# One-core hybrid mLSTM/HGRN2 step: three orders changed on ScalarE and VectorE (weight split, gate set-up, mix blocks of the output projection)

## The chip, the core and the metric

The kernel runs on one core of a Trainium2 chip. Its engines work side by side, each through its own queue of instructions in order: PE (TensorE, matrix multiplication; PEld is its weight load), DVE (VectorE), ACT (ScalarE), POOL (GpSimd) and SP (SyncE, which here issues all DMAs). A semaphore wait at the head of a queue holds everything behind it. The metric is the device time of one execution in microseconds (us), here a median of three runs: 1157.92, from 1155.51 to 1158.99.

## What is computed

One layer of a decoder trunk, on a prompt of 1024 tokens and 8 samples of 8 tokens (T = 1088 columns in all). Cut to what matters:

```python
xn = rmsnorm(x, g_norm)                                # 1024 features
xm, zm, om, fh, qh, ih, zh = split(xn @ w_in, 1024)    # 7 x 1024 outputs

xc = silu(causal_conv(xm, conv_w))                     # mLSTM: 4 heads
q, k, v = xc @ w_q, xc @ w_k, xm @ w_v                 # per head
gates = concat(q, k, v) @ w_gate + b_gate
ig, lf = gates[..., :4], log_sigmoid(gates[..., 4:])
hm, C1, n1, m1 = mlstm_scan(q / sqrt(128), k, v, ig, lf, C0, n0, m0)
hm = (layernorm(hm) * m_ln * sigmoid(om) + m_skip * xc) * silu(zm)

f = lb + (1 - lb) * sigmoid(fh)                        # HGRN2: 8 heads
oh, S1 = hgrn2_scan(silu(qh), (1 - lb) * sigmoid(-fh), ih, log(f), S0)
oh = rmsnorm(oh) * h_norm * silu(zh)

y = rmsnorm(x + concat(hm, oh) @ w_out) * g_final      # 2048 -> 1024
```

## The kernel before

**Exact products.** Each fp32 operand is kept as a rounded high part and the rest (hi, lo). A product takes three multiplications, hi·hi, lo·hi and hi·lo (`mm3`, L94 to L96). A weight block (128 x 1024) is therefore loaded raw by SP (`wraw`), copied to `whi` by ScalarE and subtracted to `wlo` by GpSimd or VectorE (`blk_split`, L147 for both). Raw blocks of W_in, of the per-head weights, of W_out (`woraw`) and of the mixed activations (`mraw`) share three buffers; whi/mhi have two, wlo/mlo two.

**The front.** For each of the four mLSTM heads, `front_conv` projects x_m in three column pieces (`in_block` with its callback: `xmh`/`XB` by ScalarE, `xml` by VectorE), and does the convolution (`Y`, L483 and L486, on VectorE) and SiLU (L492 to L498). `front_v` then computes v and the gates' share of it for nine token tiles, six multiplications each, into three PSUM buffers (tag mm, also used by the projection). ScalarE empties each with two copies: 256 columns to `vt` (L516), 8 to `GTOK` for head 0 or `GST` for the others (L517). `front_qk` computes q and k (L543). `in_block` begins, when it has a single item, with the split of the next weight block: `blk_split(nxt)`.

**Weaves and mixers.** Behind the front, `weave` interleaves projection blocks (the side list) with the mixers of HGRN2 heads and mLSTM heads in turn, H0, M0, H1 and so on to H7. From here on TensorE's order is the one in which the program is written (`manual_schedule`); the other engines' order comes from the scheduler of the framework, which takes dependencies and its own estimate of times, and a call `behind(a, b)` makes a depend on b. `gate_scan` runs beside the first mixer H0: it writes the gates to `gd` in memory and reads them back as `glf`, `gt`, `ig`, `gy` in rows, makes `lm` (4 x 8), sets eight columns of `gt` (MEMSET, L577) and of `gy` (L578), and scans (L579). At the first level H0 makes `Q` and two `K` folds on VectorE (L997, L961), then the copy `Sf` (L1012), and TensorE multiplies `lv` from them (L101).

**The output projection.** W_out is used in two halves of 512 columns, hf = 0 and 1, over token tiles t = 0 to 8 (t = 8 has 64 tokens). For each (hf, t) two groups g = 0, 1 of contraction blocks (8 and 7 blocks, 24 and 21 multiplications) are computed by `out_part`, and the last block by `out_done`, which adds x, sums squares and stores (hf = 0) or normalises and writes out y (hf = 1). `mix_prep(t, g)` loads a group's mixed activations from memory (`mixd`) into `mraw`, splits them on ScalarE (`mhi`, L1302; L1298 for t = 8) and VectorE (`mlo`, L1303). It is called at the head of each out_part, except for the very first group. `early_out` does the parts (0, 0) to (0, 4) within the last weave. What follows is the tail: out_done(0, 0..8) with parts (0, 5) to (0, 8) among them, one `wo_prep(1, i)` (load and split of a block of W_out's second half; `woh` L1276, `wol` L1277) after each of the first six, then the second half in the order 8, 0, 1, ... 7.

Of the kernel before, what the change touches and what calls it, by code (L numbers as in the profile page):

```python
# [17 lines left out]
T = 1088  # L18
# [12 lines left out]
def hybrid_step(  # L31
# [87 lines left out]
    r = 0  # L119
# [50 lines left out]
    def blk_split(i):  # L170
        if i < len(blocks):
            return w_split(("w", i), V if i in v_splits else G)
# [96 lines left out]
    def in_block(*items):  # L269


        ws = []
        for kind, j, evac in items:
            i = bidx[(kind, j)]
            if i > 1 or len(items) == 1:
                if ("w", i) in wq and not isinstance(wq[("w", i)], tuple):
                    blk_split(i)
            ws.append(i)
        for i in ws:
            blk_load(i + 2)  # L280
        nxt = ws[-1] + 1
        if len(items) == 1:
            blk_split(nxt)
        for c, (t0, n) in enumerate(CH):
            xh, xl = xchunk(XH, c), xchunk(XL, c)
            for (kind, j, evac), i in zip(items, ws):
                wh, wl = wq[("w", i)]
                ps = ps_mm()
                for k in range(8):
                    mm3(ps[:, :n], (wh[:, k, :], wl[:, k, :]), (xh[:, k, :], xl[:, k, :]), k == 0, k == 7)  # L290
                    if k % 2 and k < 7:
                        yield cost(6, n)
                evac(c, t0, n, ps)
                yield cost(6, n)
# [206 lines left out]
    def front_v(h):  # L501
        wh, wl = qkv_w[h]
        xms = [fr[2 * h + a]["m"] for a in range(2)]
        for t in range(9):
# [11 lines left out]
            S.copy(vv[:, u, 0:256], ps[:, :256])  # L516
            S.copy((GST if h else GTOK)[:, t, :], ps[:, 256:264])  # L517
            if t == 8:
# [37 lines left out]
    def gate_scan():  # L556
# [18 lines left out]
        lm = small(8, "lm")  # L575
        V.tensor_tensor(lm[0:4, :], lfs, m0t, op=ALU.add)
        V.memset(t1[:, TP:T].rearrange("p (b c) -> p b c", c=8)[:, :, 0], -1e30)  # L577
# [308 lines left out]
    def hgrn_in(h):  # L886
# [36 lines left out]
        else:  # L923
            for i in range(3):
                wo_load(0, i)
            for n, c in enumerate(in_block(("i", h, ev_i), ("z", h, ev_silu(z))), 1):
                if n == 8:
                    for i in range(3):
                        wo_split(0, i)
                    wo_load(0, 3)  # L930
                    ctxs["mix0"] = mix_prep(0, 0, True)
                elif n == 16:
                    wo_split(0, 3)
                yield c
# [6 lines left out]
    def hgrn_main(h):  # L941
# [69 lines left out]
        k2 = fold(K1[:, 512:1024], 1, 1, False)  # L1011
        V.tensor_copy(hv(Sf, T, 1)[:, :, 0, :], hv(f, T, 1)[:, :, 1, :])  # L1012
        G.memset(hv(Sf, T, 1)[:, :, 1, :], 1.0)
# [301 lines left out]

    def out_part(hf, t, g):

# [3 lines left out]
        ps = acc[(hf, t)]  # L1321
        mx = ctxs.pop("mix0") if (hf, t, g) == (0, 0, 0) else mix_prep(t, g)
        for k in range(len(mx)):
# [87 lines left out]
    def early_out():  # L1411
        for t in range(EARLY):
# [5 lines left out]
            if t < STORED:  # L1418
                out_store(t)

    side = chain(*[(hgrn_in if kind == "H" else mlstm_in)(h) for kind, h in jobs], early_out())
    prep = qkv_prep(0)
# [20 lines left out]
    with tc.manual_schedule(engines={mybir.EngineType.PE}):  # L1443
# [8 lines left out]
        weave(side, hgrn_main(7), (us / 2 + EARLY * cost(45, 512)) / HEAD["H"])  # L1452
        for t in range(9):
            out_done(0, t)
            if 3 <= t < 7:
                run(chain(out_part(0, t + 2, 0), out_part(0, t + 2, 1)))
            if t < 6:
                wo_prep(1, t)
        wo_prep(1, 6)
        wo_prep(1, 7)  # L1460
        gf = unit("gf")
        ctxs["gf"] = gf
        nc.sync.dma_start(out=gf[:, :DM], in_=g_final.unsqueeze(0).to_broadcast([P, DM]))
        for t in (8, *range(8)):
            run(chain(out_part(1, t, 0), out_part(1, t, 1)))
            out_done(1, t)
# [87 lines left out]
```

## Time and profile before

| | |
|---|---|
| three runs, median | 1157.92 us (1155.51 to 1158.99) |
| the profiled execution | 1159.27 us, of it 1157.5 us span |
| granted TensorE clock, mean | 0.992 |
| TensorE busy | 1121.6 us |
| VectorE, ScalarE, GpSimd busy | 745.1, 467.9, 259.7 us |
| DMA | 134.05 MB, 116 GB/s over the span |

A profile's timeline row is: start, duration (us), engine, line, operation, output <- inputs, partitions x elements, and how often. Brackets give the idle time of the engine before it and the instruction that ended this idle time. Durations on one engine overlap a little, since an engine begins an instruction while the one ahead drains; so the step from start to start is what counts. Line numbers are those of the kernel before.

### The profile page before, as it was taken

Reading aid. Unit: us, or ns where it says so; the run is one execution under the profiler, and the core shown is the slowest. Engines: PE = TensorE matmul, PEld = TensorE weight load, DVE = VectorE, ACT = ScalarE, POOL = GpSimd, SP = SyncE. Lnnn points to the kernel's source line nnn. Section 1 sums busy time; section 2 is a strip of 40 time slices with the busy share of each in tenths; the row PEclk is TensorE's granted clock in tenths of the full one; section 3 lists DMA queues with packets and bytes.
Section 4 is the critical chain, followed back from the end, with each engine's and each line's share of the span. In section 5 each row is a group of like instructions: output and inputs, shape, how many; then the busy total and the mean of one; then the engine's idle time right before and its main releaser. Section 6 shows DMA issues by size and latency. Waiting matters only on the chain.

```text
span 1157.5 us, 22938 instructions
## 1 busy us (share of the span) xinstructions
PE 1121.6 (97%) x9251; PEld 1055.4 (91%) x9251; DVE 745.1 (64%) x1474; ACT 467.9 (40%) x1045; POOL 259.7 (22%) x403
## 2 busy tenths in 40 slices
PE   5889999999999999999999999999999999999997
PEld 5789999899999999999999999999999997878886
DVE  4665354394778667784779567877676686644543
ACT  5454454434532444235423453252524354333332
POOL 4352443102530044203530153102020200100000
PEclk9889999999999999999999999999999999999999
DMA  7234343213324152323224331422222255576662
GB/s 250 56 122 143 119 144 126 71 50 117 103 76 146 54 167 73 122 94 127 64 78 151 116 112 60 133 76 77 56 77 56 76 175 144 156 215 177 188 190 93
DMA packets 154296, 134.05 MB, mean 116 GB/s; under 512 B 11515, under 2 KB 130391, under 8 KB 154190
## 3 DMA queue, kind: packets, MB, share of 16 engines
q1 hardware_dynamic: 154190, 132.59, 36.6%
q8 instruction: 73, 1.20, 0.4%
q14 instruction: 33, 0.27, 0.1%
HBM read 93.99 MB, written 38.57 MB: 115 GB/s over the span
## 4 chain that ended last, share of the span: by engine, by line
PE 84%; DVE 6%; DMA 5%; ACT 3%; issue 2%; POOL 0%; SPq 0%; POOLq 0%; DVEq 0%; ACTq 0%
PE mm L94 23%; PE mm L95 23%; PE mm L96 23%; PE lv L101 2%; DMA mraw<-mixd 2%; DMA woraw<-in_w_out 2%; PE o L1190 1%; PE o L1209 1%; PE o L94 1%; PE o L96 1%; PE o L95 1%; PE o L1212 1%; DVE mlo L1303 1%; PE lv L1171 1%; PE o L1104 1%
## 5 line engine op out<-in xcount | busy, mean ns | idle before, releaser
L94 PE MATMUL mm<-XH,whi 128*128 128x384 f32 (+1 forms) x1344 | 450.1, 335 | 2.2 <-DVE xml L470 2.0
L95 PE MATMUL mm<-XL,whi 128*128 128x384 f32 (+1 forms) x1344 | 440.0, 327 | 0.0
L96 PE MATMUL mm<-XH,wlo 128*128 128x384 f32 (+1 forms) x1344 | 439.5, 327 | 0.0
L94 PEld LDWEIGHTS mm<-XH,whi 128*128 128x128 f32 x1344 | 253.8, 189 | 4.8 <-DVE xml L470 2.2
L95 PEld LDWEIGHTS mm<-XL,whi 128*128 128x128 f32 x1344 | 253.7, 189 | 1.6 <-issue 1.3
L96 PEld LDWEIGHTS mm<-XH,wlo 128*128 128x128 f32 x1344 | 253.2, 188 | 0.0
L147 POOL TENSOR_TENSOR wlo<-wraw,whi 128x1024 fp32r<-128x1024 f32 x34 | 83.1, 2445 | 104.7 <-ACT whi L147 104.6
L147 ACT CAST whi<-wraw 128x1024 fp32r<-128x1024 f32 x56 | 58.8, 1050 | 94.5 <-PE mm L95 74.6
L948 POOL MEMSET A<- 128x288 f32 x8 | 2.7, 343 | 261.4 <-ACT A L1077 261.4
L1302 ACT CAST mhi<-mraw 128x1024 fp32r<-128x1024 f32 (+1 forms) x32 | 31.8, 997 | 66.5 <-PE mm L95 42.8
L96 PE MATMUL mm<-XH,mlo 128*128 128x512 f32 x144 | 56.5, 392 | 2.1 <-DVE mlo L1303 2.1
L94 PE MATMUL mm<-XH,mhi 128*128 128x512 f32 x144 | 56.9, 395 | 1.2 <-ACT mhi L1302 1.2
L95 PE MATMUL mm<-XL,mhi 128*128 128x512 f32 x144 | 56.1, 390 | 0.0
L1303 DVE TENSOR_TENSOR mlo<-mraw,mhi 128x1024 fp32r<-128x1024 f32 (+1 forms) x32 | 37.0, 1156 | 20.6 <-ACT mhi L1302 19.4
L470 DVE TENSOR_TENSOR xml<-mm,xmh 128x384 fp32r<-128x384 f32 (+1 forms) x24 | 12.3, 511 | 50.9 <-ACT XB L469 47.9
L896 DVE TENSOR_SCALAR f<-f,OML,LB 128x384 f32<-128x384 f32 (+1 forms) x24 | 32.8, 1368 | 12.0 <-ACT f L894 11.6
L1371 POOL TENSOR_TENSOR rs<-rs,mhalf 128x1 f32<-128x1 f32 (+1 forms) x9 | 4.9, 542 | 148.5 <-DVE rs L1370 148.5
L96 PE MATMUL mm<-woh,mlo 128*128 128x512 f32 x96 | 37.5, 390 | 0.1
L95 PE MATMUL mm<-wol,mhi 128*128 128x512 f32 x96 | 37.4, 389 | 0.0
L94 PE MATMUL mm<-woh,mhi 128*128 128x512 f32 x96 | 37.3, 389 | 0.0
L486 DVE SCALAR_TENSOR_TENSOR Y<-XB,PAR,Y 128x1112 f32<-128x1112 f32 x24 | 36.8, 1533 | 0.3
L964 DVE TENSOR_TENSOR QK<-hk,Sf 128x256 f32<-128x256 f32 x96 | 36.2, 419 | 0.0
(355 smaller groups left out, 2188.3 us busy)
## 6 DMA issues: line engine op xcount, KB each, us to landing
wraw<-in_w_in SPq DMA_DIRECT2D x56, 512.0 KB
woraw<-in_w_out SPq DMA_DIRECT2D x16, 512.0 KB
mraw<-mixd SPq DMA_DIRECT2D x16, 512.0 KB
mraw<-mixd SPq DMA_DIRECT2D x16, 448.0 KB
xcd<-XB SPq DMA_DIRECT2D x8, 544.0 KB
qkd<-qk SPq DMA_DIRECT2D x16, 272.0 KB
xcr<-xcd SPq DMA_DIRECT2D x8, 544.0 KB
mixd<-xcr SPq DMA_DIRECT2D x8, 544.0 KB
```

The source lines that it names most:

```text
L94: PE.matmul(out, lhsT=lh, rhs=rh, start=first, stop=False)
L95: PE.matmul(out, lhsT=lh, rhs=rl, start=False, stop=False)
L96: PE.matmul(out, lhsT=ll, rhs=rh, start=False, stop=last)
L101: i = PE.matmul(out, lhsT=lhsT, rhs=rhs, start=start, stop=stop)
L147: return S.copy(hi, raw), eng.tensor_tensor(lo, raw, f32(hi), op=ALU.subtract)
L470: evs.append(V.tensor_tensor(ml[:, t0:t0 + m], ps[:, :m], f32(mh[:, t0:t0 + m]), op=ALU.subtract))
L486: V.scalar_tensor_tensor(Y[:, :1112], XB[:, j:j + 1112], cw[:, 8 * j + ft:8 * j + ft + 1], Y[:, :1112], op0=ALU.mult, op1=ALU.add)
L896: V.tensor_scalar(f[:, s], f[:, s], scalar1=OML[:, h:h + 1], scalar2=LB[:, h:h + 1], op0=ALU.mult, op1=ALU.add)
L964: i = V.tensor_tensor(dst, ksrc, ssrc, op=ALU.mult)
L1104: PE.transpose(pt[:, u * P:(u + 1) * P], iT[:, t * P:(t + 1) * P], ident)
L1302: S.copy(hi[:, :w * n], raw[:, :w * n])
L1303: V.tensor_tensor(lo[:, :w * n], raw[:, :w * n], f32(hi[:, :w * n]), op=ALU.subtract)
```

## The change

Three edits. (a) Where a block has a single item, ScalarE's copy of the next block's whi is made to depend on the copy that front_v makes to GTOK or GST for its second token tile (t = 1), if one was noted; the note is used up, so this concerns one block per mLSTM head. (b) `lm` in gate_scan is made to depend on the copy Sf of the HGRN2 mixer's first level. (c) In the tail, out_part prepares the mix of the next group before it multiplies its own, from a table of what comes next; the parts come first and the out_done calls behind them, two after each part, with a wo_prep behind each of the first six; and the load of g_final stands ahead of the loop.

```diff
--- before.py
+++ after.py
@@ -280,7 +280,9 @@
             blk_load(i + 2)
         nxt = ws[-1] + 1
         if len(items) == 1:
-            blk_split(nxt)
+            r = blk_split(nxt)
+            if "v1" in ctxs:
+                behind(r[0], ctxs.pop("v1"))
         for c, (t0, n) in enumerate(CH):
             xh, xl = xchunk(XH, c), xchunk(XL, c)
             for (kind, j, evac), i in zip(items, ws):
@@ -514,7 +516,9 @@
                 mm3(ps[:, :264], (xms[a][0][:, t * P:(t + 1) * P], xms[a][1][:, t * P:(t + 1) * P]),
                     (wh[:, o:o + 264], wl[:, o:o + 264]), a == 0, a == 1)
             S.copy(vv[:, u, 0:256], ps[:, :256])
-            S.copy((GST if h else GTOK)[:, t, :], ps[:, 256:264])
+            gc = S.copy((GST if h else GTOK)[:, t, :], ps[:, 256:264])
+            if t == 1:
+                ctxs["v1"] = gc
             if t == 8:
                 nc.sync.dma_start(out=vsd[h], in_=vt[:, :VW])
             elif u:
@@ -573,7 +577,7 @@
         lfs = lf[:, TP:T].rearrange("p (b c) -> p b c", c=8)[:, :, 0]
         igs = ig[:, TP:T].rearrange("p (b c) -> p b c", c=8)[:, :, 0]
         lm = small(8, "lm")
-        V.tensor_tensor(lm[0:4, :], lfs, m0t, op=ALU.add)
+        behind(V.tensor_tensor(lm[0:4, :], lfs, m0t, op=ALU.add), ctxs["k2"])
         V.memset(t1[:, TP:T].rearrange("p (b c) -> p b c", c=8)[:, :, 0], -1e30)
         V.tensor_tensor(y[:, TP:T].rearrange("p (b c) -> p b c", c=8)[:, :, 0], igs, lm[0:4, :], op=ALU.max)
         V.tensor_tensor_scan(m, t1, y, initial=0.0, op0=ALU.add, op1=ALU.max)
@@ -928,7 +932,7 @@
                     for i in range(3):
                         wo_split(0, i)
                     wo_load(0, 3)
-                    ctxs["mix0"] = mix_prep(0, 0, True)
+                    ctxs["mixes"][0, 0, 0] = mix_prep(0, 0, True)
                 elif n == 16:
                     wo_split(0, 3)
                 yield c
@@ -1009,7 +1013,7 @@
 
         k1 = fold(K1[:, 0:512], 1, 0, False)
         k2 = fold(K1[:, 512:1024], 1, 1, False)
-        V.tensor_copy(hv(Sf, T, 1)[:, :, 0, :], hv(f, T, 1)[:, :, 1, :])
+        ctxs["k2"] = V.tensor_copy(hv(Sf, T, 1)[:, :, 0, :], hv(f, T, 1)[:, :, 1, :])
         G.memset(hv(Sf, T, 1)[:, :, 1, :], 1.0)
         V.tensor_tensor(hv(f, T, 1)[:, :, 1, :], hv(f, T, 1)[:, :, 1, :], hv(f, T, 1)[:, :, 0, :], op=ALU.mult)
         yield 5.0
@@ -1313,13 +1317,17 @@
                 else:
                     PE.matmul(ps, lhsT=mx, rhs=w[1], start=False, stop=False)
 
-    def out_part(hf, t, g):
+    mixes = {}
+
+    def out_part(hf, t, g, ahead=None):
 
         n = ntok(t)
         if g == 0:
             acc[(hf, t)] = ps_mm()
         ps = acc[(hf, t)]
-        mx = ctxs.pop("mix0") if (hf, t, g) == (0, 0, 0) else mix_prep(t, g)
+        mx = mixes.pop((hf, t, g), None) or mix_prep(t, g)
+        if ahead:
+            mixes[ahead] = mix_prep(*ahead[1:])
         for k in range(len(mx)):
             stop = hf == 0 and t < STORED and (g, k) == (1, 6)
             mm_out(ps, t, mx[k], wo[(hf, g * 8 + k)], g == 0 and k == 0, stop)
@@ -1418,6 +1426,7 @@
             if t < STORED:
                 out_store(t)
 
+    ctxs["mixes"] = mixes
     side = chain(*[(hgrn_in if kind == "H" else mlstm_in)(h) for kind, h in jobs], early_out())
     prep = qkv_prep(0)
     next(prep)
@@ -1450,19 +1459,30 @@
                 main, extra = with_gates(main, gates), 11.5
             weave(islice(side, STEPS), main, us / (HEAD[kind] + extra))
         weave(side, hgrn_main(7), (us / 2 + EARLY * cost(45, 512)) / HEAD["H"])
-        for t in range(9):
-            out_done(0, t)
-            if 3 <= t < 7:
-                run(chain(out_part(0, t + 2, 0), out_part(0, t + 2, 1)))
-            if t < 6:
-                wo_prep(1, t)
-        wo_prep(1, 6)
-        wo_prep(1, 7)
+        parts = [(0, t) for t in range(EARLY, 9)] + [(1, 8)] + [(1, t) for t in range(8)]
+        nexts = [(*p, g) for p in parts for g in range(2)]
+        nexts = dict(zip(nexts, nexts[1:] + [None]))
+        mixes[0, EARLY, 0] = mix_prep(EARLY, 0)
+
+        def part_of(hf, t):
+            for g in range(2):
+                run(out_part(hf, t, g, nexts[hf, t, g]))
+
         gf = unit("gf")
         ctxs["gf"] = gf
         nc.sync.dma_start(out=gf[:, :DM], in_=g_final.unsqueeze(0).to_broadcast([P, DM]))
+        wos = iter(range(6))
+        for t in range(EARLY, 9):
+            part_of(0, t)
+            for n in (t - 1, t - EARLY):
+                out_done(0, n)
+                for i in islice(wos, 1):
+                    wo_prep(1, i)
+        wo_prep(1, 6)
+        out_done(0, 8)
+        wo_prep(1, 7)
         for t in (8, *range(8)):
-            run(chain(out_part(1, t, 0), out_part(1, t, 1)))
+            part_of(1, t)
             out_done(1, t)
```

The order of ScalarE around the first tiles of v of mLSTM head 1, before (mm_1016 is the last piece of the projection, mm_1063 and mm_1075 the first two tiles of v):

```order
L147 CAST whi_1182<-wraw_954 128x1024
L468 CAST xmh_952<-mm_1016 128x256
L469 COPY XB_949<-mm_1016 128x256
L516 COPY vt_1064<-mm_1063 128x256
L517 COPY GST<-mm_1063 128x8
L516 COPY vt_1064<-mm_1075 128x256
L517 COPY GST<-mm_1075 128x8
```

And now:

```order
L470 CAST xmh_952<-mm_1016 128x256
L471 COPY XB_949<-mm_1016 128x256
L518 COPY vt_1064<-mm_1063 128x256
L519 COPY GST<-mm_1063 128x8
L474 COPY XB_949<-mm_1016 128x8x8
L475 CAST xmh_952<-mm_1016 128x128
L518 COPY vt_1064<-mm_1075 128x256
L519 COPY GST<-mm_1075 128x8
L147 CAST whi_1182<-wraw_954 128x1024
```

The weight split whi_1182 went behind the second GST copy; XB and xmh from mm_1016 went ahead of the second tile's copies. Heads 2 and 3 look the same, and at head 0 the split went behind the second GTOK copy.

The order of VectorE at the first level of H0, before:

```order
L576 TENSOR_TENSOR lm_2448<-glf_2330,m0t 4x8
L586 COPY glf_2330<-lm_2448 4x8
L577 MEMSET gt_2331 4x8
L578 TENSOR_TENSOR gy_2329<-ig_2328,lm_2448 4x8
L147 TENSOR_TENSOR wlo_2367<-wraw_2241,whi_2366 128x1024
L904 TENSOR_TENSOR hq_2051<-hq_2051,mm_2301 128x320
L997 TENSOR_TENSOR Q_316_2353<-hq_2051,f_2049 128x544
L961 COPY K_317_2356<-hk_2050 128x256
L961 COPY K_317_2356<-hk_2050 128x4x64
L1012 COPY Sf_2352<-f_2049 128x544
L579 SCALAR_TENSOR_TENSOR gm_2332<-gt_2331,gy_2329 4x1088
```

And now:

```order
L581 MEMSET gt_2331 4x8
L147 TENSOR_TENSOR wlo_2367<-wraw_2241,whi_2366 128x1024
L908 TENSOR_TENSOR hq_2051<-hq_2051,mm_2301 128x320
L1001 TENSOR_TENSOR Q_316_2353<-hq_2051,f_2049 128x544
L965 COPY K_317_2356<-hk_2050 128x256
L965 COPY K_317_2356<-hk_2050 128x4x64
L1016 COPY Sf_2352<-f_2049 128x544
L580 TENSOR_TENSOR lm_2448<-glf_2330,m0t 4x8
L1018 TENSOR_TENSOR f_2049<-f_2049 128x544
L582 TENSOR_TENSOR gy_2329<-ig_2328,lm_2448 4x8
L590 COPY glf_2330<-lm_2448 4x8
L583 SCALAR_TENSOR_TENSOR gm_2332<-gt_2331,gy_2329 4x1088
```

The set-up of the gates (lm, gy, glf) and the scan (gm) stand behind Sf; the MEMSET of gt stays ahead of wlo. The multiplication of f by itself is now ahead of the scan.

The order of ScalarE in the tail, before (woh: a block of W_out's second half; mhi 1024 and 896: groups 0 and 1 of a token tile; L1358 the sums of squares of out_done), from the fourth woh on:

```order
L1276 CAST woh_11806<-woraw_11804 128x1024
L1358 ACTIVATE lv_11715,SS<-xr_11232 128x512
L1358 ACTIVATE lv_11729,SS<-xr_11487 128x512
L1358 ACTIVATE lv_11743,SS<-xr_11487 128x512
L1302 CAST mhi_11822<-mraw_11820 128x1024
L1276 CAST woh_11879<-woraw_11877 128x1024
L1302 CAST mhi_11852<-mraw_11850 128x896
L1358 ACTIVATE lv_11816,SS<-xr_11810 128x512
L1276 CAST woh_11952<-woraw_11950 128x1024
L1302 CAST mhi_11895<-mraw_11893 128x1024
L1302 CAST mhi_11925<-mraw_11923 128x896
```

And now, from the preparation of group (0, 6, 0) on:

```order
L1306 CAST mhi_11737<-mraw_11735 128x1024
L1306 CAST mhi_11794<-mraw_11792 128x896
L1280 CAST woh_11860<-woraw_11858 128x1024
L1366 ACTIVATE lv_11768,SS<-xr_11762 128x512
L1366 ACTIVATE lv_11782,SS<-xr_11232 128x512
L1280 CAST woh_11874<-woraw_11872 128x1024
L1306 CAST mhi_11824<-mraw_11822 128x1024
L1306 CAST mhi_11881<-mraw_11879 128x896
L1280 CAST woh_11946<-woraw_11944 128x1024
L1366 ACTIVATE lv_11855,SS<-xr_11849 128x512
L1366 ACTIVATE lv_11869,SS<-xr_11232 128x512
L1280 CAST woh_11960<-woraw_11958 128x1024
```

Before, one woh stands between the mhi of (0, 6, 0) and of (0, 6, 1), and one ahead of both mhi of tile 7. Now both mhi of a tile stand together, and two woh behind them, so that a woh's wait for its load falls behind the mhi of the same tile and ahead of the next tile's. On SP's queue the loads stand accordingly: mix blocks (0, 5, 0), (0, 5, 1) and (0, 6, 0) and g_final ahead of the first two blocks of W_out, then two mix blocks and two blocks of W_out in turn.

## The prediction

> **What bounds the kernel now.** I read the page first, then the waits of TensorE (engine, line, what it waited for: total us, times, longest us), then timelines of four places.
>
> ```profile
> span 1157.5 us, 22938 instructions
> PE 1121.6 (97%) x9251; PEld 1055.4 (91%) x9251; DVE 745.1 (64%) x1474; ACT 467.9 (40%) x1045; POOL 259.7 (22%) x403
> PE 84%; DVE 6%; DMA 5%; ACT 3%; issue 2%; POOL 0%; SPq 0%; POOLq 0%; DVEq 0%; ACTq 0%
> PE lv L241 <- DVE xsq L229: 12.4, 4, 9.7
> PE mm L94 <- DVE wqh L414: 3.3, 1, 3.3
> PE lv L101 <- DVE K L961: 2.3, 1, 2.3
> PE mm L96 <- DVE mlo L1303: 2.1, 3, 1.0
> PE mm L94 <- ACT GST L517: 1.3, 3, 0.4
> PE mm L94 <- ACT mhi L1302: 1.2, 1, 1.2
> ```
>
> TensorE is busy for 97% of the span, and the change takes no matrix multiplication away. So it can win only what TensorE waits. The 12.4 us at the start (x's norm) is not touched. The next five rows are the places that the change works on: 3.3 + 2.3 + 2.1 + 1.3 + 1.2 = 10.2 us. That is the whole stake, 0.9% of the span. It comes in four terms: the front of head 0, the front of heads 1 to 3, the first level of the first HGRN2 mixer, the tail.
>
> **The fronts of heads 1 to 3.** ScalarE, GpSimd and TensorE at head 1; a bracket gives the idle time before and who ended it:
>
> ```profile
> 104.77 1.05 ACT L147 CAST whi<-wraw 128x1024 fp32r<-128x1024 f32 x1 [2.50 <-PE mm L95]
> 105.72 0.37 ACT L468 CAST xmh<-mm 128x256 fp32r<-128x256 f32 x1
> 106.25 0.39 ACT L516 COPY vt<-mm 128x256 f32<-128x256 f32 x1
> 106.51 0.19 ACT L517 COPY GST<-mm 128x8 f32<-128x8 f32 x1
> 104.72 0.28 PE L94 MATMUL mm<-wqh,xmh 128*128 128x264 f32 x1
> 106.05 0.28 PE L96 MATMUL mm<-wqh,xml 128*128 128x264 f32 x1
> 106.75 0.39 PE L94 MATMUL mm<-wqh,xmh 128*128 128x264 f32 x1 [0.42 <-ACT GST L517]
> 112.03 0.28 PE L96 MATMUL mm<-wqh,xml 128*128 128x264 f32 x1
> ```
>
> v's first two tiles take 12 multiplications from 104.72 to 106.05, so one step is (106.05 − 104.72)/11 = 0.121 us. The third tile starts 0.70 after the last of them instead of 0.12: **0.58 us lost**, since its PSUM buffer is emptied by the copies to vt and GST, and these stand behind the weight split `whi` (0.95 from start to start). The change puts `whi` behind the second tile's GST copy. Then xmh starts at about 104.9 instead of 105.72 (its product is there by then), the first GST ends at 106.70 − 0.8 = 105.9, before the 106.17 at which the third tile wants it. The 0.58 goes. The split now holds up the copies of the third tile by 0.95: they end at about 108.1, and the sixth tile, next to use that buffer, is due at 104.72 + 30 × 0.121 = 108.35. That is enough, by 0.25.
>
> All nine tiles (54 steps, 6.55 us) take 7.43 from 104.72 to 112.15, so at most 0.88 can go per head. The rest beyond 0.58 is waits of 0.1 or less for later tiles, which fall away if ScalarE's copies keep ahead; I take 0.73 for each head. The waits view counts three such waits, one for each of heads 1 to 3: **3 × 0.73 = 2.2 us**, bounds 1.7 (3 × 0.58) and 2.6.
>
> What moves along: the subtraction `wlo` on GpSimd starts 1 to 1.5 us later, and the raw block behind it is loaded that much later by SP's queue. The block split at 104.77 belongs to the projection block after next: once v is done, TensorE first runs a whole block whose weights are split already, 72 multiplications of 320 to 384 columns, at least 72 × 0.121 = 8.7 us. That hides it; without this cover it would cost the same 1 to 1.5 us per head.
>
> **The front of head 0.**
>
> ```profile
> 56.55 3.17 POOL L147 TENSOR_TENSOR wlo<-wraw,whi 128x1024 fp32r<-128x1024 f32 x1 [0.33 <-ACT whi L147]
> 56.15 1.36 DVE L486 SCALAR_TENSOR_TENSOR Y<-XB,PAR,Y 128x1112 f32<-128x1112 f32 x1
> 57.77 3.12 DVE L486 SCALAR_TENSOR_TENSOR Y<-XB,PAR,Y 128x1112 f32<-128x1112 f32 x1
> 61.45 0.78 PE L94 MATMUL mm<-wqh,xmh 128*128 128x264 f32 x2 [3.27 <-DVE wqh L414]
> 67.74 0.17 ACT L517 COPY GTOK<-mm 128x8 f32<-128x8 f32 x1
> 67.96 0.39 PE L94 MATMUL mm<-wqh,xmh 128*128 128x264 f32 x1 [0.23 <-ACT GTOK L517]
> 77.36 2.53 POOL L498 TENSOR_TENSOR xcl<-XB,xch 128x1088 fp32r<-128x1088 f32 x1 [6.35 <-ACT xch L497]
> 85.09 0.41 ACT L543 ACTIVATE qk<-mm 128x272 f32<-128x272 f32 x1
> 57.00:61.40 4.40, 0.29 (x2) 0.20 (x2) 4.40 (x6) 0.16 (x3) 3.93 (x2) 0.89 0.43 127
> 61.40:67.20 5.80, 5.16 (x22) 4.91 (x23) 3.60 (x6) 3.79 (x8) 1.12 (x1) 0.50 0.25 75
> ```
>
> (The last two are rows by stretch: length, then busy time of PE, PEld, DVE, ACT, POOL, granted clock, DMA share, GB/s.) The step L486 takes 1.36 us alone and 3.12 while GpSimd subtracts `wlo` (3.17 there): the two lay over each other and neither ran at its own speed. With `wlo` put off, the second L486 should take 1.36, and `wqh` be ready 1.76 us earlier, so TensorE starts v at 59.7. But v is not bound by TensorE here. Its tiles wait for ScalarE, whose queue holds the SiLU work of the convolution, and what is 1.76 earlier is the second tile's GTOK (67.91 → 66.15). Behind it now stands `whi`, which gives 0.95 back: the third tile's copies end some 0.8 earlier than before, and from there on TensorE sets the pace with steps of 0.121. The tile that waits for these copies began 6 steps behind the 67.96, at 68.7, and can now begin at 67.5. Between 0.8 and 1.2 I take **1.0 us** for head 0, bounds 0 (L486 stays long, for GpSimd's next piece lies there) and 1.8 (nothing given back).
>
> A rule of the Trainium skill ("SBUF — State Buffer", section "Who interferes with whom") bears on the long L486: a VectorE instruction with two inputs in SBUF and a GpSimd instruction that reads SBUF exclude each other on a shared port. The rows of 3.12 and 3.17 agree. By that rule the moved `wlo` only looks for another victim: it would meet the L486 steps of the next convolution tile and cost them the same 1.76 us. That is rival (3); the rule leaves the sum as it is as long as TensorE doesn't wait for that tile.
>
> **The granted clock** fell to 0.50 behind this idle stretch, from 61.4 to 67.2. A shorter idle stretch might keep it up; since ScalarE sets v's pace there, I count nothing. The Trainium skill ("TensorE: Matmul & The Clock Gate", section "What's actually happening") puts the drop after one idle window of about 3.4 us. The 3.27 us of the row agree roughly, and by that rule v's first tiles would now run at full speed, for the reason given again without a change of the sum.
>
> **The first level.** DVE and TensorE in the first HGRN2 mixer:
>
> ```profile
> 227.95 0.07 DVE L577 MEMSET gt<- 4x8 f32 x1 [0.77 <-DMA gt<-gd]
> 228.63 0.16 DVE L578 TENSOR_TENSOR gy<-ig,lm 4x8 f32<-4x8 f32 x1 [0.62 <-DMA gy<-gd]
> 229.12 1.23 DVE L147 TENSOR_TENSOR wlo<-wraw,whi 128x1024 fp32r<-128x1024 f32 x1 [0.32 <-issue]
> 232.05 0.65 PE L101 MATMUL lv<-Q,K 128*32 128x64 f32 x32 [2.27 <-DVE K L961]
> ```
>
> The gates' set-up (lm, glf, gt, gy) waits on VectorE for DMAs out of gd, and behind it stands wlo, hq, Q, K, for which TensorE waits 2.27. The change holds lm behind the copy Sf, and the order shows that gy and the scan go with it; but the MEMSET of gt, which waits for the same round trip, stays at the head. So wlo starts at 228.05 instead of 229.12: **1.05 us**, not 2.27. Bounds 0.8 and 2.3 (if TensorE's whole wait went). The scan (2.40) now starts after the multiplication on f; who needs the gates next is the first mLSTM mixer, a whole weave later.
>
> **The tail.** ACT, DVE, TensorE, and two links of the chain of waits:
>
> ```profile
> 1033.80 1.05 ACT L1276 CAST woh<-woraw 128x1024 fp32r<-128x1024 f32 x1 [6.35 <-DMA woraw<-in_w_out]
> 1034.75 1.88 ACT L1302 CAST mhi<-mraw 128x1024 fp32r<-128x1024 f32 x2
> 1036.02 1.22 DVE L1303 TENSOR_TENSOR mlo<-mraw,mhi 128x1024 fp32r<-128x1024 f32 x1
> 1034.01 0.39 PE L95 MATMUL mm<-XL,zh 128*128 128x512 f32 x1
> 1034.24 0.39 PE L96 MATMUL mm<-XH,zl 128*128 128x512 f32 x1
> 1035.84 0.50 PE L94 MATMUL mm<-XH,mhi 128*128 128x512 f32 x1 [1.22 <-ACT mhi L1302]
> 1037.29 0.50 PE L96 MATMUL mm<-XH,mlo 128*128 128x512 f32 x1 [0.71 <-DVE mlo L1303]
> 1027.66 6.11 DMA woraw<-in_w_out
> 1057.38 3.95 DMA mraw<-mixd
> ```
>
> Token tile 7's mix is split (mhi, then mlo) behind a block of W_out that ScalarE waited 6.35 us for. From 1034.24 to 1037.29 lie three steps, 3 × 0.23 = 0.69 us of work in 3.05: **2.36 us lost**. With mixes prepared one group ahead, mhi of tile 7 stands ahead of that block, so all of it goes; the part and the final block of the next tile (45 + 3 multiplications, 11.0 us) lie between the preparation and its use. Against it: in the last tile order (1,8), (1,0), (1,1) the mix ahead stands closer to the read-back of the sums stored before, and I charge 0.1. Tail **2.25 us**, bounds 0 and 2.4. The load of g_final (512 KB) that moves forward is one transfer and lies in the cover of a whole part.
>
> **Sum:** 1.0 + 2.2 + 1.05 + 2.25 = 6.5 us. The profiled run took 1159.27 (span 1157.5 and 1.8 around it), so it would be 1152.8; it lies 1.35 above the median of the three runs, so the median becomes 1157.92 − 6.5 = **1151.4 us**.
>
> **Rivals.**
>
> (1) The tail's wait only moves. For three tiles the loop now fetches two blocks of W_out and two of the mix per tile over three raw buffers. Each buffer is held for a transfer and a split: 2 × 6.11 + 2 × 3.95 + 4 × (1.05 + 1.22) = 29.2 us, over three buffers 9.7 per tile, against TensorE's 45 + 6 steps of 0.23 = 11.7. For it: 2 us is a thin margin, and transfers get longer when two run together. If each transfer takes 1.9 us more, it is 12.2 and TensorE waits 0.5 per tile; at 2.5 more, 13.1, which costs 1.4 × 3 = 4.2 and gives 1155.6. Between the two I price it at the tail's 2.25 lost: 1157.92 − 4.25 = 1153.7. Chance 0.17.
>
> (2) Slower: one of the three raw buffers is tied up. A mix that is loaded a group ahead keeps its buffer until its split, and that split waits for one of two mhi buffers, which TensorE frees only at the end of a group. If one is so held all the time, two buffers carry the four loads: 29.2/2 = 14.6 us per tile against 11.7, 2.9 × 3 = 8.7 us, and the 2.25 is not won: 1157.92 − 4.25 + 8.7 = 1162.4. It decides once the held time of a mix passes 3 × 11.7 − 29.2 = 5.9 us per tile. Against it: TensorE frees an mhi each 5 us. Chance 0.06.
>
> (3) Head 0 gives nothing, since another GpSimd piece falls on L486, and the moved `wlo` costs the next chain its time: 1157.92 − 5.5 = 1152.4; if the next tile's chain, with its xcl, then came late for q and k, up to 1.8 more, 1154.2. Against it: xcl ended at 79.89 and the first q product was copied out at 85.09, some 0.8 us of multiplying after TensorE wanted xcl, so about 4 us are free. Chance 0.10.
>
> (4) It does more than I count: all of the first level's 2.3 and head 0's 1.8: 1157.92 − 8.6 = 1149.3. Chance 0.12.
>
> **Chances.** Forecast 0.55, rivals 0.17, 0.06, 0.10, 0.12. A measurement of this kernel can tell about 0.3% (3.5 us) from no change, so faster means below 1154.4. The forecast, (4) and nearly all of (3) lie there, and half of (1): 0.55 + 0.12 + 0.09 + 0.08 = 0.84, less 0.06 for the spread of the runs (1155.51 to 1158.99): 0.78; slower is (2), 0.06; same the rest, 0.16. The range goes from a little past (4), 1148, to the middle of (1), 1155.3.
>
> **What would show it.** In the profile after: no wait of TensorE for GST; wqh's wait shorter by 1.5 to 2; K's wait 1.0 to 1.5 instead of 2.3; no wait for mhi near part (0,7). It is wrong if the waits for mlo, mhi or woh between part (0,6) and (1,1) add up to over 2 us (rival 1), or to over 8 (rival 2), or if L486 still shows a 3 us step ahead of wqh (rival 3).

## The result and the profile after

The kernel after takes **1149.70 us** (median of five runs, 1148.73 to 1151.14) against 1158.99 for the kernel before in the same comparison: ratio 0.9916, 95% interval 0.9903 to 0.9929, that is 8.2 to 11.2 us less. The forecast of 1151.4 (1148.0 to 1155.3) held, with a gain that was larger than the 6.5 us worked out. The profiled execution has a span of 1148.0 us, 9.5 below that of before.

The page of after, and then the waits of TensorE (engine, line, waited for: total us, times, longest):

```profile
span 1148.0 us, 22950 instructions
PE 1118.2 (97%) x9251; PEld 1053.7 (92%) x9251; DVE 748.1 (65%) x1474; ACT 468.3 (41%) x1045; POOL 262.0 (23%) x403
PE 89%; DVE 5%; DMA 2%; ACT 2%; issue 1%; POOL 0%; SPq 0%; POOLq 0%; DVEq 0%; ACTq 0%
```

```profile
PE mm L94 <- DVE wqh L416: 1.4, 1, 1.4
PE mm L94 <- ACT GTOK L519: 1.2, 2, 0.9
PE lv L101 <- DVE K L965: 1.0, 1, 1.0
PE mm L96 <- DVE mlo L1307: 0.4, 1, 0.4
```

The waits for GST and mhi are gone, those for wqh, K and mlo are 1.9, 1.3 and 1.7 us shorter. One wait grew by 1.0: GTOK, 1.2 us at head 0, where it had been 0.2. DMA's share of the chain (the third line of the page) fell from 5% to 2%. At head 1 the order is the one that was meant, and the third tile of v starts 0.12 us behind the last multiplication of the second, at 104.35:

```profile
104.21 0.17 ACT L519 COPY GST<-mm 128x8 f32<-128x8 f32 x1
105.00 1.07 ACT L147 CAST whi<-wraw 128x1024 fp32r<-128x1024 f32 x1
104.47 0.35 PE L94 MATMUL mm<-wqh,xmh 128*128 128x264 f32 x1
```

In the tail the mhi of token tile 7 is done 3.7 us before TensorE comes to it (1022.80 and 1026.53):

```profile
1020.80 1.05 ACT L1280 CAST woh<-woraw 128x1024 fp32r<-128x1024 f32 x1 [0.97 <-DMA woraw<-in_w_out]
1021.75 1.05 ACT L1306 CAST mhi<-mraw 128x1024 fp32r<-128x1024 f32 x1
1026.53 0.39 PE L94 MATMUL mm<-XH,mhi 128*128 128x512 f32 x1
```

### Where the time went, stage by stage

All kernels of this study run the same 9251 multiplications, and up to the tail in nearly the same order (with edit (a) some ten at head 0 change places). The same ones lie ahead of each of seven fixed multiplications in every trace, so the starts of these seven, and the stretches between them, can be compared. The first row has the lengths in the profile of before, the others the difference to it, in us (worked out from the start times of multiplications number 226, 500, 1090, 1350, 1700, 8290, 8600 and the last of each trace):

| kernel | x's norm, first block | head 0 | heads 1-3 | gates | first level | mixers | last weave | tail |
|---|---|---|---|---|---|---|---|---|
| before | 54.78 | 48.76 | 87.50 | 36.49 | 30.39 | 701.93 | 40.65 | 149.79 |
| **after** | −0.70 | −1.00 | −2.42 | 0.01 | −1.31 | −0.29 | −0.87 | −2.91 |
| after again | −1.99 | −1.02 | −2.42 | 0.01 | −1.47 | −0.03 | −1.34 | −2.79 |
| (a) alone | 1.08 | −1.00 | −2.40 | −0.01 | −0.42 | 0.33 | −1.51 | −0.74 |
| (b) alone | −0.13 | 0.03 | 0.01 | −0.01 | −1.32 | −0.12 | −1.12 | 0.53 |
| (c) alone | 2.25 | −0.01 | −0.02 | 0.00 | 1.35 | −0.29 | 0.08 | −2.53 |
| wlo alone | 1.96 | −1.75 | 0.00 | 0.00 | 1.52 | 0.88 | −1.31 | −0.32 |
| after, fourth tile | 1.77 | −1.56 | −2.40 | −0.01 | −1.18 | 0.57 | −1.65 | −2.91 |
| after, MEMSET behind | −0.28 | −1.01 | −2.40 | −0.01 | −2.35 | −0.01 | −1.71 | −2.79 |
| after, no mix ahead | 1.91 | −1.01 | −2.40 | −0.01 | 3.21 | −0.06 | −1.99 | −2.22 |
| after, old tail order | 1.39 | −1.01 | −2.40 | −0.01 | −1.23 | 0.67 | −1.11 | −1.99 |

Read it by columns. In "head 0" and "heads 1-3" kernels with the same front agree within 0.04 us: there the table measures edits. In the first column no kernel differs from another, yet the entries spread over 4.2 us; in "mixers" and "last weave" they spread over 1.2 and 2.1 without any pattern of the edits. So of the 9.5 us, 1.00 + 2.42 + 1.31 + 2.91 = **7.6 lie where the edits are**, and 0.70 + 0.29 + 0.87 = 1.9 in stages that move by themselves. The first level and the tail move too where no edit acts on them (−0.42 to 1.52 and −0.74 to 0.53), so for these two a single pair of profiles is a rough measure.

### The profile page after: what moved, and what is told of

It is laid out like the page before. It is cut to its first block, busy times and chain, and to the rows that moved or that the text cites. A ratio compares the mean times of both kernels' runs of the same rounds, so it can differ in the third digit from the quotient of the medians.

```text
span 1148.0 us, 22950 instructions
## 1 busy us (share of the span) xinstructions
PE 1118.2 (97%) x9251; PEld 1053.7 (92%) x9251; DVE 748.1 (65%) x1474; ACT 468.3 (41%) x1045; POOL 262.0 (23%) x403
## 4 chain that ended last, share of the span: by engine, by line
PE 89%; DVE 5%; DMA 2%; ACT 2%; issue 1%; POOL 0%; SPq 0%; POOLq 0%; DVEq 0%; ACTq 0%
PE mm L94 24%; PE mm L95 24%; PE mm L96 24%; PE lv L101 2%; PE o L1194 1%; PE o L1213 1%; PE o L94 1%; PE o L95 1%; PE o L96 1%; PE o L1216 1%; DMA mraw<-mixd 1%; PE lv L1175 1%; PE o L1108 1%; PE mm L1316 1%; PE mm L1318 1%
## 5 line engine op out<-in xcount | busy, mean ns | idle before, releaser
L147 POOL TENSOR_TENSOR wlo<-wraw,whi 128x1024 fp32r<-128x1024 f32 x34 | 85.6, 2519 | 82.2 <-ACT whi L147 82.1
L488 DVE SCALAR_TENSOR_TENSOR Y<-XB,PAR,Y 128x1112 f32<-128x1112 f32 x24 | 43.1, 1796 | 0.3
```

The source lines that it names most:

```text
L147: return S.copy(hi, raw), eng.tensor_tensor(lo, raw, f32(hi), op=ALU.subtract)
L488: V.scalar_tensor_tensor(Y[:, :1112], XB[:, j:j + 1112], cw[:, 8 * j + ft:8 * j + ft + 1], Y[:, :1112], op0=ALU.mult, op1=ALU.add)
```

## The experiments

### Each edit alone

Before, with only the lines of edit (a), (b) or (c) of the change.

```diff
 (a)  in_block: behind(r[0], ctxs.pop("v1")); front_v: note the copy of t == 1
 (b)  gate_scan: behind(lm, ctxs["k2"])
 (c)  out_part(..., ahead), mixes, the new tail loop
```

> Edit (a) alone: ScalarE's weight split behind the second v tile, the rest as before. Theory (the four edits' gains lie at their own places and add up): TensorE gains 1.2 to 1.9 us at the front of head 0 and 0.6 to 0.9 at each of heads 1 to 3, nothing behind 200 us; together 3.3 to 4.3 us, the ratio to before 0.9965 +- 0.001. Rival (the front's gain is lost again at the next fixed wait, so that it only pays with the other edits): the wait for K at the first level grows by what the front gained, and the total is within 1 us of before.

> Edit (b) alone: lm behind the copy Sf. Theory: TensorE's wait for K at the first level falls from 2.3 to 1.0 to 1.3 us and all else stays, 1.0 to 1.3 us in all, ratio 0.999. The wait for mlo in the last weave (1.0 us before, gone after) stays at about 1.0 here if it belongs to edit (c) or to chance. Rival: the set-up of the gates comes later and the first mLSTM mixer waits for it: new waits between 240 and 330 us.

> Edit (c) alone: the mix blocks one group ahead and the tail in its new order. Theory: all before 950 us stays; the tail gains 2.4 to 2.9 us (the waits for mhi and mlo at token tile 7 and the small one at part (1, 0)); ratio 0.9975. If the wait for mlo in the last weave is also gone here, it is edit (c)'s; if it is there, it came from the earlier edits or from chance. Rival: loads of W_out crowd the mix blocks: waits of over 1 us for woh, mhi or mlo behind 1000 us.

Measured, as ratios of the times to before (95% interval): (a) 0.9956 (0.9940 to 0.9973), (b) 0.9979 (0.9967 to 0.9990), (c) 0.9971 (0.9959 to 0.9984). The three multiplied make 0.9906, and the whole change 0.9916, well within what their intervals leave open: **the edits add up** as far as the times can tell. In the table each pays at its own place: (a) 3.40 at the four heads, (b) 1.32 at the first level, (c) 2.53 in the tail. Of (a), 1.00 lies at head 0, less than the 1.2 to 1.9 that I expected there. The rivals fall: with (a) alone the wait for K did not grow by the front's gain, with (b) no new wait appeared between 240 and 330 us (one of 0.6 for S, as before), with (c) no wait of TensorE stood behind 1000 us.

Two things fit worse. With (a) alone the first level is also 0.42 shorter, though nothing there was changed: counted from the fixed multiplication ahead of it, wlo starts 0.42 us earlier (1.16 against 1.58), behind the same read-backs out of gd, so the round trip came in sooner. And the wait for mlo in the last weave (1.4 us in two waits before) was 0.2 and 0.4 with (a) and (b) alone and 1.5 with (c) alone; with wlo alone it was 0.4. No edit acts there, so I take its part in the result (1.0 us of waits, 0.87 of the stage) for chance; no run shows what sets it.

### What made head 0 late: the weight split's place or GpSimd's subtraction

Before, with only `wlo` held back, not `whi` (shown against edit (a)):

```diff
             r = blk_split(nxt)
             if "v1" in ctxs:
-                behind(r[0], ctxs.pop("v1"))
+                behind(r[1], ctxs.pop("v1"))
```

> Before, with only GpSimd's wlo of the front's blocks held behind the second v tile's small copy; ScalarE's copy whi stays where it was. Port theory (the long convolution step is GpSimd's subtraction lying over it): at head 0 the second step L488 takes 1.36 us instead of 3.12, wqh comes about 1.7 us earlier and TensorE gains 1.5 to 1.9 there; heads 1 to 3 keep their wait of 0.4 us for GST (0.58 from start to start), so nothing there. Queue theory (it is whi's place on ScalarE that makes head 0 late): L488 stays near 3 us and head 0 gains under 0.5.

Measured: 0.9986 (0.9973 to 0.9999). DVE, POOL and TensorE of this kernel at head 0, and TensorE at head 1:

```profile
59.73 1.35 DVE L488 SCALAR_TENSOR_TENSOR Y<-XB,PAR,Y 128x1112 f32<-128x1112 f32 x1
62.83 2.37 POOL L147 TENSOR_TENSOR wlo<-wraw,whi 128x1024 fp32r<-128x1024 f32 x1
67.45 6.37 DVE L488 SCALAR_TENSOR_TENSOR Y<-XB,PAR,Y 128x1112 f32<-128x1112 f32 x3
61.65 0.48 PE L94 MATMUL mm<-wqh,xmh 128*128 128x264 f32 x2 [1.50 <-DVE wqh L416]
106.97 0.39 PE L94 MATMUL mm<-wqh,xmh 128*128 128x264 f32 x1 [0.42 <-ACT GST L519]
```

The second L488 went from 3.12 to 1.35 us with `whi` where it was, wqh's wait from 3.27 to 1.50, and head 0 gained 1.75 us; heads 1 to 3 kept their 0.42 for GST. So the two parts of edit (a) act apart: **head 0 is won by moving GpSimd's work off VectorE's, heads 1 to 3 by moving ScalarE's copy.** At head 0 the moved `whi` even costs something: 1.00 with it against 1.75 without. Here wlo fell into a gap and ran in 2.37 us. In after it does not. POOL and DVE of after:

```profile
57.40 1.35 DVE L488 SCALAR_TENSOR_TENSOR Y<-XB,PAR,Y 128x1112 f32<-128x1112 f32 x1
64.97 8.36 DVE L488 SCALAR_TENSOR_TENSOR Y<-XB,PAR,Y 128x1112 f32<-128x1112 f32 x3
65.38 3.35 POOL L500 TENSOR_TENSOR xcl<-XB,xch 128x1088 fp32r<-128x1088 f32 x1 [6.55 <-ACT xch L499]
68.69 3.47 POOL L147 TENSOR_TENSOR wlo<-wraw,whi 128x1024 fp32r<-128x1024 f32 x1
77.10 2.54 POOL L500 TENSOR_TENSOR xcl<-XB,xch 128x1088 fp32r<-128x1088 f32 x1 [4.93 <-ACT xch L499]
83.37 0.41 ACT L547 ACTIVATE qk<-mm 128x272 f32<-128x272 f32 x1
```

The three L488 of the next convolution tile take 8.36 us instead of 6.37, and xcl and wlo on GpSimd lie over them: the victim changed, and pays 2.0 us. That agrees with the rule of the Trainium skill ("SBUF — State Buffer", section "Who interferes with whom"), by which a VectorE instruction with two inputs in SBUF contends with a GpSimd instruction that reads SBUF. It costs nothing, since xcl still ends at 79.64 and q is copied out at 83.37, and TensorE does not wait for xcl.

### What the split gives back at head 0

After, with the note taken at t == 3 instead of t == 1.

```diff
-            if t == 1:
+            if t == 3:
                 ctxs["v1"] = gc
```

> After, with the split whi behind the copies of v's fourth tile instead of the second. Theory (whi still stands between the copies of two tiles and gives back a little at head 0): the second wait for GTOK at head 0 (0.3 us) goes, TensorE gains 0.2 to 0.4 there against after, heads 1 to 3 stay within 0.2, the first GTOK wait (0.9) stays, since it is xch that stands ahead of it. Rival (whi's place gives nothing back, the copies have room): no change at head 0, and wlo that comes later still costs the next convolution tile its time, with a new wait for xcl before 90 us.

ScalarE and TensorE of after, at head 0 (third tile: the copies behind `whi`):

```profile
65.53 1.06 ACT L147 CAST whi<-wraw 128x1024 fp32r<-128x1024 f32 x1
66.48 0.38 ACT L518 COPY vt<-mm 128x256 f32<-128x256 f32 x1
66.74 0.18 ACT L519 COPY GTOK<-mm 128x8 f32<-128x8 f32 x1
65.69 0.39 PE L94 MATMUL mm<-wqh,xmh 128*128 128x264 f32 x1 [0.90 <-ACT GTOK L519]
66.98 0.39 PE L94 MATMUL mm<-wqh,xmh 128*128 128x264 f32 x1 [0.30 <-ACT GTOK L519]
```

With the fourth tile the 0.30 is gone and the first wait (0.98) stays; head 0 gains 1.56 instead of 1.00, heads 1 to 3 the same 2.40. So 0.56 is what `whi` gave back behind the second tile, more than the 0.2 to 0.4 that I expected. The interval of the ratio to before, 0.9927 (0.9903 to 0.9951), is too wide to show it.

### What is left of the wait for K

After, with the MEMSET behind Sf as well.

```diff
-        V.memset(t1[:, TP:T]..., -1e30)
+        behind(V.memset(t1[:, TP:T]..., -1e30), ctxs["k2"])
```

> After, with the MEMSET of gt held behind the copy Sf too, so that no instruction that waits for the round trip through gd stands ahead of wlo on VectorE. Theory (the MEMSET is what keeps 1.0 us of TensorE's wait for K): the wait falls to 0.3 or less, 0.7 to 1.0 us less than after, ratio to before 0.9905. Rival (K waits for hq's product or for wlo itself): the wait stays at about 1.0.

VectorE and TensorE of after, then VectorE of this kernel:

```profile
223.63 0.07 DVE L581 MEMSET gt<- 4x8 f32 x1 [3.10 <-DMA gt<-gd]
223.70 1.23 DVE L147 TENSOR_TENSOR wlo<-wraw,whi 128x1024 fp32r<-128x1024 f32 x1
226.64 0.65 PE L101 MATMUL lv<-Q,K 128*32 128x64 f32 x32 [0.97 <-DVE K L965]
```

```profile
222.91 1.23 DVE L147 TENSOR_TENSOR wlo<-wraw,whi 128x1024 fp32r<-128x1024 f32 x1 [1.96 <-ACT whi L147]
226.07 0.07 DVE L581 MEMSET gt<- 4x8 f32 x1
```

As forecast, wlo starts right behind the MEMSET in after. Without the MEMSET ahead it starts when its whi is there, and TensorE doesn't wait for K at all: the first level is 2.35 shorter than before instead of 1.31. The ratio is 0.9911 (0.9898 to 0.9924); against the 0.9916 of after, the times do not show the gain.

### Which half of the tail's edit counts

After, once without the mix ahead, and once with the tail's old order:

```diff
 (no mix ahead)
-        mixes[0, EARLY, 0] = mix_prep(EARLY, 0)
-                run(out_part(hf, t, g, nexts[hf, t, g]))
+                run(out_part(hf, t, g))
 (old tail order, with the mix ahead; cut: the new loop goes, the load of g_final stands behind)
+        for t in range(9):
+            out_done(0, t)
+            if 3 <= t < 7:
+                part_of(0, t + 2)
+            if t < 6:
+                wo_prep(1, t)
```

> After, with the tail in the new order but without the mix one group ahead: each group's mix is loaded and split when its turn comes, behind the blocks of W_out. Theory (it is the mix ahead that takes the tail's wait away): 2 us or more of waits for mhi and mlo come back between parts (0, 5) and (1, 1). Rival (it is the order of parts, final blocks and W_out's loads): waits there stay under 0.7 us as in after.

> After, with the mix one group ahead but the tail in its old order (final blocks 0 to 3 with three W_out blocks first, then part, final block, W_out block in turn). Theory (the mix ahead is what counts): waits for mhi and mlo in the tail stay under 0.7 us. Rival (order): ScalarE still has a block of W_out that waits for its load ahead of the mhi of a tile, and 1 to 2.4 us of wait stay at token tile 7.

Here my theory fell. Without the mix ahead no wait for mhi or mlo came back in the tail, and with the mix ahead in the old order 0.34 us did, at part (1, 0). The tail gains 2.22 us by the order alone, 1.99 by the mix ahead alone, and 2.7 to 2.9 by both in the five profiles of the whole change with this tail: **either half takes most of the wait away, and they don't add.** In the tail without the mix ahead, ScalarE and TensorE:

```profile
1018.68 1.05 ACT L1280 CAST woh<-woraw 128x1024 fp32r<-128x1024 f32 x1 [6.02 <-DMA woraw<-in_w_out]
1019.64 1.89 ACT L1306 CAST mhi<-mraw 128x1024 fp32r<-128x1024 f32 x2
1021.71 0.39 PE L94 MATMUL mm<-XH,mhi 128*128 128x512 f32 x1
```

A block of W_out still holds ScalarE up for 6.02 us ahead of two mhi. But in this order a whole part is multiplied before the first blocks of W_out are asked for, and TensorE has work in hand until 1021.71: the first of the two mhi (token tile 6) is done at 1020.69, 1.0 us before that, where after has 3.7 us to spare at tile 7.

The late block of W_out costs something at another place, though. At the end of the last HGRN2 mixer, inside the tail's stretch of the table, TensorE waits 0.34 us for the state S in this kernel, and 0.92 us in the next one with this tail (the run with the MEMSET behind, below). VectorE and TensorE of the latter:

```profile
998.85 1.12 DVE L1248 SCALAR_TENSOR_TENSOR S<-S,f,o 128x128 f32<-128x128 f32 x4 [1.89 <-PE o L1245]
1000.98 1.23 DVE L1281 TENSOR_TENSOR wol<-woraw,woh 128x1024 fp32r<-128x1024 f32 x1 [1.01 <-ACT woh L1280]
1002.13 1.12 DVE L1248 SCALAR_TENSOR_TENSOR S<-S,f,lv 128x128 f32<-128x128 f32 x4
1003.39 0.30 PE L1175 MATMUL lv<-CF,osq 128*128 128x128 f32 x1 [0.92 <-DVE S L1248]
```

The split wol, which waits for its block, stands between the two sets of S; in after these follow each other, and no profile but the two without the mix ahead has this wait. Without it the order alone would have gained about 2.5 us in both (an estimate: 2.22 + 0.34 and 1.55 + 0.92), as much as (c) alone.

The ratios are 0.9951 (0.9937 to 0.9964) without the mix ahead and 0.9933 (0.9921 to 0.9945) in the old order. The first is 4 us above after, and its tail doesn't explain that. Its first level does, in the profile. VectorE and TensorE there, and then a row by stretch (length, busy PE, PEld, DVE, ACT, POOL, granted clock, DMA share, GB/s):

```profile
228.26 0.07 DVE L581 MEMSET gt<- 4x8 f32 x1 [5.13 <-DMA gt<-gd]
231.28 1.08 PE L101 MATMUL lv<-Q,K 128*32 128x64 f32 x32 [3.01 <-DVE K L965]
```

```profile
231.00:237.00 6.00, 5.72 (x93) 5.72 (x94) 6.00 (x15) 0.83 (x5) 1.99 (x6) 0.50 0.29 85
```

The instructions are those of after in the same order, but SP could issue the read-back of gt only 2.0 us later, behind the write it waits for. TensorE waited 3.01 us instead of 0.97, and its granted clock was 0.50 for the next six: in all 3.21 − (−1.31) = 4.5 us lost behind one late transfer.

### The round trip taken out, and after once more

Both halves of the tail's edit again, with the MEMSET behind Sf; the fourth tile and the MEMSET together; and after, unchanged, beside them.

> The tail in its new order without the mix ahead (the run before with this tail was 4 us slower than after, with no wait in its tail but 4.5 us lost at the first level, where the MEMSET waited for a late round trip), and now the MEMSET behind Sf. Theory (that loss was the round trip, and the tail's order alone takes the tail's wait away): no wait for K, none over 0.7 us for mhi or mlo in the tail, time within 1.5 us of after in the same batch. Rival (the tail without the mix ahead is slower in most executions, and the profile was a lucky one): still 3 us or more above after.

> The mix ahead with the tail's old order, and the MEMSET behind Sf. Theory (either half of edit (c) takes most of the tail's wait away): waits for mhi and mlo in the tail of 0.4 to 1.0 us in all, no wait for K, time 0.3 to 1.5 us above the run with the new tail and the MEMSET behind Sf (0.9911 of before). Rival: 2 us or more of waits in the tail.

> After, with both additions: whi behind v's fourth tile, and the MEMSET of gt behind the copy Sf. Theory (the two lie at different places and add): against after 0.3 to 0.5 us at head 0 and 1.0 us or more at the first level; no wait for K, one wait for GTOK; ratio to before 0.990, 1 to 2 us below after in the same batch. Rival (what is left there is chance of the round trip and of the clock): the same as after within 0.5 us.

> After, unchanged, beside the others on the same chip. Theory (the wait for K that is left depends on when the round trip through gd lands): it lies anywhere from 1.0 to 3.0 us; above about 2.2 us TensorE's granted clock falls behind it and 1 to 2.5 us more go. Rival: 1.0 us as before, and the clock stays up.

| kernel | median us | ratio to before | first level | tail |
|---|---|---|---|---|
| no mix ahead, MEMSET behind | 1151.42 | 0.9926 (0.9909 to 0.9943) | −2.35 | −1.55 |
| old tail order, MEMSET behind | 1150.56 | 0.9919 (0.9899 to 0.9939) | −2.34 | −2.07 |
| fourth tile, MEMSET behind | 1149.72 | 0.9910 (0.9894 to 0.9927) | −2.35 | −2.73 |
| after again | 1151.07 | 0.9915 (0.9899 to 0.9931) | −1.47 | −2.79 |

Without the MEMSET ahead the first level is the same within 0.01 us in all four kernels that have it so, and the kernel without the mix ahead stands 0.35 us from after instead of 4. That speaks for the round trip as most of what set it apart, though the two intervals (0.9937 to 0.9964 and 0.9909 to 0.9943) overlap a little. After again had a wait for K of 0.83, a little below the 1.0 that I gave as the least, and its clock stayed up; one profile doesn't show how often a longer wait comes. The tail without the mix ahead gained least in its second profile (1.55 after 2.22), by the wait for S. The fourth tile with the MEMSET has the shortest stages where the edits are (head 0 −1.56, first level −2.35; together 1.6 us less than after), and its median is 1.35 below after's in that batch, but the intervals overlap: faster than after is not shown by the times.

## Why the prediction was right

**What bounds the kernel.** Right: the gain is waits of TensorE, and each edit's gain was found at the wait that the waits view had named. But the stake of 10.2 us was counted too high: of the 2.1 us for mlo 1.4 lay in the last weave, where no edit acts. The tail's term was worked out from its own rows and is not touched by that.

**Heads 1 to 3.** 2.2 forecast, 2.42 measured: 0.81 a head, close to the 0.88 that nine tiles in steps of 0.121 left. The room of 0.25 that I found behind the moved split was enough: no wait for GST is left.

**Head 0.** 1.0 forecast, 1.00 measured, and by the mechanism that was put down: L486 goes from 3.12 to 1.35, worth 1.75 by the run with wlo alone, then a part is given back, 0.75. Of that 0.56 is the place of `whi` between two tiles, by the fourth-tile run; the other 0.19 no run takes apart. That the number came out to the hundredth is luck: 1.0 was picked between 0.8 and 1.2. Not foreseen was that xml now goes ahead of gv on VectorE, which lengthens TensorE's wait for gv from 1.4 to 1.7. That the moved wlo would meet the next convolution tile's L486 was right, and so was the room there. That v's first tiles might run at full speed was not: the granted clock fell again, to 0.50 for 3.4 us in after and for 6.8 us in (a) alone and in after again, as in before (from 60.45, while TensorE still waited for wqh). As argued it makes no difference to head 0, which gains 1.00, 1.00 and 1.02 us in the three; TensorE waits for GTOK there, that is, for ScalarE.

**First level.** 1.05 forecast, 1.31 and 1.47 measured. That the MEMSET stays ahead and keeps 1 us was read from the order of the instructions, not from the diff, and the run with the MEMSET behind Sf shows it.

**The tail.** 2.25 forecast with 2.4 as the upper end, 2.5 to 2.9 measured in six profiles: the term was too small, and what came lies beyond its upper bound. I left out a small wait at part (1, 0), 0.30 from start to start in the trace of before, and charged 0.1 for a read-back that cost nothing. The old tail also moves by itself: the other three profiles that keep it lie between −0.74 and 0.53. And the reason given, the mix one group ahead, is only half of it: the order alone does nearly as much. In after the mhi of tile 7 stands ahead of the block that held it up, but behind two others, for which ScalarE waited 3.02 and 0.97 us; it comes in time because TensorE still has 3.7 us of work in hand. Rivals (1) and (2) put the price of the loads at up to 8.7 us; no profile of the whole new tail shows a wait of TensorE for woh, mhi or mlo there. Only without the mix ahead does a late block of W_out reach TensorE, by the 0.34 and 0.92 us for S.

**The sum.** 6.5 forecast, 7.6 where the edits are, and 9.3 between the medians, with an interval from 8.2. By the time alone rival (4) came nearer (1149.3, a gain of 8.6), but not by its terms: head 0 gave 1.00 and not 1.8, the first level 1.31 and not 2.3. What lies beyond 7.6 is not at any edit's place in the profiled pair, so that the time still fell into the range owes something to chance. One candidate: of the four profiles that keep the old order at the first level, two ((c) alone and wlo alone) are 1.35 and 1.52 us longer there than before, with the granted clock at 0.50 for 3.4 us behind the wait for K, and none of the five with lm behind Sf, the MEMSET ahead and a read-back in time is. Edit (b) would then be worth more on average than in the profile of before, which lost nothing to the clock there; its time alone, 1.2 to 3.8 us, fits. It is argued, since most timed executions left no profile.

## What to carry to other kernels

Read the order of the queues, not only the edit: what still waits at the head of an in-order queue (here one MEMSET of 4 x 8 elements) decides how much of a wait goes. Where an instruction of one engine takes twice its usual time, look for what lies beside it on GpSimd, and ask where that work will fall if it is moved. And where two kernels run the same multiplications in the same order, compare the start of the same one: stages that differ by 0.01 us and stages that differ by 2 us without an edit tell effect from chance better than whole times do.

## What the runs showed of the hardware

TensorE's granted clock can fall behind a wait of little more than 2 us, and need not. TensorE's first multiplication behind K in (c) alone, the stretch behind it, and the same stretch in before:

```profile
234.36 1.08 PE L101 MATMUL lv<-Q,K 128*32 128x64 f32 x32 [2.35 <-DVE K L961]
```

```profile
234.40:237.00 2.60, 2.60 (x83) 2.56 (x84) 2.60 (x3) 0.51 (x4) 0.06 (x1) 0.50 0.56 163
```

```profile
232.10:235.00 2.90, 2.90 (x91) 2.87 (x92) 2.90 (x3) 0.52 (x4) 0.37 (x1) 1.00 0.50 149
```

So after 2.35 us it was 0.50, after 2.27 us in before 1.00. At the same place it was 0.50 after 3.01 us (no mix ahead) and after 2.22 us (wlo alone, for 3.4 us), and it did not fall after 1.85 us ((a) alone) or after 0.8 to 1.1 us. The clock records of the traces offer a reason. Before the last multiplications every stretch at 0.50 is 3.4 or 6.8 us long, and within one execution all begin on one grid of 3.41 us: in (c) alone at 42.85, 63.33 and 234.00, that is 6 and 50 steps apart. On that grid the wait in (c) alone put 1.98 us of idle time into one step, at whose end the clock fell, while the 2.27 us in before were cut into 1.34 and 0.93. The other two that fell had 1.95 and 1.92 us in a step, and (a) alone, which didn't, had 1.64. This is a reading of one place, and no run tests it; at the start of the program it doesn't hold (in before the clock fell at 39.97, behind a step with 0.57 us idle).

The Trainium skill ("TensorE: Matmul & The Clock Gate", section "What's actually happening") speaks of one idle window of about 3.4 us that runs freely; the runs agree with a free-running window, but the waits that set it off here are shorter than that.

The round trip through memory (136 KB written, rows of 17 KB read back), from the instruction that makes `lg` to the MEMSET that waits for it, took 5.3 to 5.7 us from start to start in nine profiles and 7.5 in one. And the first 54.8 us of the program, in which no kernel differs from another, took 52.8 to 57.0 us over the profiles.

**Still open:** why the kernel without the mix ahead was 4 us slower in the median and not in one execution alone. Its profile shows the late round trip, and with the MEMSET behind Sf the median came within 0.35 us of after, but whether its other executions lost their time at the same place no profile tells.
